# Gate and up columns of the last feed forward as a 2x2 block product in 7 products

## The chip, the cores and the metric

The kernel runs on one core of a Trainium2 chip. The metric is the device time of one execution in microseconds (us). Five engines matter: TensorE (PE in the profile, PEld its weight loads), VectorE (DVE), ScalarE (ACT), GpSimd (POOL) and the queue of SyncE (SPq), which issues the transfers.

## The reference

Two transformer layers on 512 tokens of width 1024, with 256 context tokens. Each layer has a mixer (attention and others) and a feed forward. The change is in the feed forward of layer 1, the last stage of the kernel:

```python
def modulate(x, g, shift, scale):
    return rmsnorm(x, g) * (1.0 + scale) + shift

def swiglu(h, wg, wu, wd):
    return (jax.nn.silu(h @ wg) * (h @ wu)) @ wd
```

Here h is 512 x 1024, wg and wu are 1024 x 2816 (22 column tiles of 128), wd is 2816 x 1024. Everything is f32.

## The kernel before

Activations lie transposed: a tile has 128 features on the partitions and tokens along its length. Every f32 operand of a matmul is split into a high part (H, a cast to fp32r on ACT or POOL) and a low part (L, the rest, a subtraction on DVE), and `mm3` (L141) makes a product of three matmuls: H by H, H by L, L by H. All stages use it.

A weight tile goes through one path. `load` (L122) takes one of four slots of a ring (`wrp`, 128 x 1024 f32) and issues a transfer on SP's queue; `split` (L127) casts it on ACT (L131) and subtracts on DVE (L132). The slot is free once both are done.

The feed forward (`ffn`, L426) goes through the 22 columns in chunks, for layer 1 of 8, 8 and 6 (`CHUNKS1`). For a column j it loads the gate tile wg[j] and the up tile wu[j] (128 x 1024: 8 blocks of 128 x 128, k = 0 to 7), and for each half of the tokens (256 each, `HALVES`) makes gate and up: 2 halves x 2 x 8 x 3 = 96 matmuls of 256 columns. Gate and up of a half share a PSUM bank (`ps_one` for half 0, `ps_tp` for half 1). ACT takes the Silu (L459), DVE multiplies by up (L460), ACT and DVE split the result into aH and aL (L461). The first two columns are interleaved (`lead=2`): both on half 0, then both on half 1. After a chunk of n columns come its 8 down tiles: n x 3 matmuls of 512 columns each into a bank, and a residual on DVE (L322). In the last chunk each residual is followed by the store of that tile.

Ahead of it stands the norm (`last_norm`, L1287), once per half, when the output product of the mixer is done for it (`mix_out`): square sums, a matmul with ones (L279), the reciprocal root, and R, the factor per token in PSUM (L287). `modulated` (L290) then makes for each of 8 k: nt = x R on DVE (L295), scale and shift on ACT (L296), hH on POOL (L297) and hL on DVE (L90). Half 1's norm lies beside the first columns on half 0.

The order of instructions on each engine is set when the program is built, by a scheduler that follows the tile framework's dependences; tiles of a pool are handed round in turn, and each engine runs its instructions in that order.

Of the kernel before, what the change touches and what calls it, by code (L numbers as in the profile page):

```python
# [16 lines left out]
P = 128  # L17
# [24 lines left out]
def trunk(ctx: ExitStack, tc: tile.TileContext, A: dict, out: bass.AP):  # L42
# [23 lines left out]
    def ps_one(shape):  # L66
        return ps.tile(shape, F32, tag="one", name="ps_one", bufs=4)
# [7 lines left out]
    def slot3(dt, name="s3"):  # L75
        return base.tile([P, TT], dt, tag="x3", name=name, bufs=12)
# [12 lines left out]
    def sub(dst, a, H):  # L89
        return dve.tensor_tensor(dst, a, H.bitcast(F32), op=ALU.subtract)  # L90
# [47 lines left out]
    def cut(w, n):  # L138
        return [(w[0][:, 128 * i:128 * i + 128], w[1][:, 128 * i:128 * i + 128]) for i in range(n)]

    def mm3(o, a, b, first, last):  # L141
        (aH, aL), (bH, bL) = a, b
        pe.matmul(o, aH, bH, start=first, stop=False)  # L143
        pe.matmul(o, aH, bL, start=False, stop=False)  # L144
        return pe.matmul(o, aL, bH, start=False, stop=last)  # L145

    waiting, blocks = [], [0]

# [81 lines left out]
    def mod(layer, cond, i):  # L230
        return mods[layer][:, cond, 8 * i:8 * i + 8]
# [40 lines left out]
    def rstd_of(xs, sl, slot=lambda name: slot3(F32, name), between=lambda: None):  # L272

        n = sl.stop - sl.start
        nt = n // 128
        acc = square_sum(xs, sl, slot)
        pt = ps_tp([P, 4, 2])
        for i in range(nt):
            pe.matmul(pt[:, i, :], acc[:, 128 * i:128 * i + 128], ones[:, 0:2], start=True, stop=True)  # L279
        r = small.tile([P, 8], F32, tag="rq", name="rq")  # L280
        between()
        rsqrt(r[:, :nt], pt[:, :nt, 0], 1.0 / 1024, TABR)
        diag = slot("diag")
        for i in range(nt):
            dve.tensor_scalar(diag[:, 128 * i:128 * i + 128], ident, r[:, i:i + 1], None, op0=ALU.mult)
        R = ps_pv([P, 512])
        pe.matmul(R[:, :n], ones, diag[:, :n], start=True, stop=True)  # L287
        return R

    def modulated(xs, sl, R, a, sh, h, ks=range(KT), at=0):  # L290
        n = sl.stop - sl.start
        for k in ks:
            t = slot3(F32, name="nt")
            H, L = h[k][0][:, at:at + n], h[k][1][:, at:at + n]
            dve.tensor_tensor(t[:, :n], xs[k][:, sl], R[:, :n], op=ALU.mult)  # L295
# [130 lines left out]
    def ffn(layer, xs, groups, chunks, last, background=None, grouped=None, ends=None, lead=1, pre=None, nbuf=(2, 1)):  # L426


        off, last_of = 0, []
        nmax = max(n for _, n in chunks)  # L430
        with ExitStack() as own:
            fp = own.enter_context(tc.tile_pool(name=f"ffn{layer}", bufs=1, side="left"))
            more = own.enter_context(tc.tile_pool(name=f"fws{layer}", bufs=1, side="right"))
            turn = [0]

            def ws_unit(src, cols):

                turn[0] += 1
                if (turn[0] - 1) % sum(nbuf) < nbuf[0]:
                    return unit(src, cols, pre, bufs=nbuf[0])  # L440
                return unit(src, cols, more, bufs=nbuf[1])

            def columns(js, acts):
                ws, sgs = [], []
                for j in js:
                    ws.append([cut(ws_unit(A[w + str(layer)][j], 1024), KT) for w in ("wg", "wu")])
                    sgs.append(slot3(F32, name="sg"))
                    acts.append(tuple(fp.tile([P, TT], F32R, tag="a" + x, name="a" + x, bufs=nmax) for x in "HL"))
                for gi, (sl, _, h) in enumerate(groups):
# [12 lines left out]

            for ci, (j0, nj) in enumerate(chunks):
                final = ci == len(chunks) - 1
                if background and final:
                    background.end()
                acts = []
                j = j0
                while j < j0 + nj:
                    js = range(j, j + (lead if j == 0 else 1))  # L470
                    columns(js, acts)
                    j = js.stop
                    if background and j == lead:
                        with tc.issue_after(last_of[1].ins):
                            background.start()
                            background.step()
                    elif background and not final:
                        background.step()

                def wunit(m, unit=ws_unit, **kw):  # L480
                    c = 128 * nj
                    o = (off + m * nj * 128) * 128
                    return cut(unit(A[f"wd{layer}"][o:o + 128 * c].rearrange("(p c) -> p c", p=P), c, **kw), nj)

                def down(pt, w, m, sl, cond):
                    n = sl.stop - sl.start
                    feature_gemm(pt[:, :n], w, [(a[:, sl], b[:, sl]) for a, b in acts])
                    residual(pt[:, :n], xs[m], sl, mod(layer, cond, 5)[:, m:m + 1])

                if final and grouped:  # L490
                    with tc.tile_pool(name=f"fwr{layer}", bufs=1, side="left") as rp:
                        ws = []
                        for gi, (sl, cond) in enumerate(ends):
                            for m in range(KT):
                                if len(ws) <= m:
                                    kw = dict(unit=unit, hp=rp, tag="wd", bufs=KT - sum(nbuf)) if m < KT - sum(nbuf) else {}
                                    ws.append(wunit(m, **kw))
                                down(ps_one([P, 512]), ws[m], m, sl, cond)
                            grouped(gi)
                elif len(groups) == 2 and groups[0][1] == groups[1][1]:  # L500
                    whole = slice(groups[0][0].start, groups[1][0].stop)
                    for m in range(KT):
                        down(ps_one([P, 512]), wunit(m), m, whole, groups[0][1])
                        if final:
                            last(m)
                else:
                    for m in range(KT):
                        w = wunit(m)
                        for sl, cond, _ in groups:
                            down(ps_one([P, 512]), w, m, sl, cond)  # L510
                off += nj * 8 * 128

    def wo_unit(layer, m, hp, bufs):
# [771 lines left out]
    a_ffn = scale_cols(1, 0, 4, "norm_ffn1")  # L1285

    def last_norm(i):  # L1287
        R = rstd_of(xs, HALVES[i])
        h[i] = new_h(1 - i)
        modulated(xs, HALVES[i], R, a_ffn, mod(1, 0, 3), h[i])  # L1290

    banks(3)
    pre1 = ctx.enter_context(tc.tile_pool(name="pre1", bufs=1, side="right"))
    with tc.tile_pool(name="wo1", bufs=1, side="right") as wp:
        mix_out(1, mixs, xs, [(sl, 0, [(H[:, sl], L[:, sl]) for H, L in mixs]) for sl in HALVES], wp, last_norm, wo1)

    def store(m):
        sp.dma_start(out=out[m], in_=xs[m][:, MAIN])

    ffn(1, xs, [(HALVES[i], 0, [(H[:, :256], L[:, :256]) for H, L in h[i]]) for i in range(2)], CHUNKS1, store, lead=2, pre=pre1, nbuf=(4, 1))  # L1300


PARCOLS, ROWCOLS = {}, {}
# [143 lines left out]
```

## Time and profile before

| | |
|---|---|
| median of 3 runs | 1772.79 us (1772.67 to 1772.89) |
| the profiled execution | 1770.36 us, span of its instructions 1768.5 us |
| mean granted TensorE clock | 0.984 |
| PE, DVE, ACT, POOL busy | 1695.4, 945.3, 634.4, 253.3 us |
| last stage (feed forward of layer 1) on PE | from 1392.35 us on |

The times in the profile are those of the one profiled execution, counted from its first instruction. Busy times are sums over the whole span; what a stage costs is read from its own stretch. DVE, ACT and POOL have much idle time in the last stage.

### The profile page before, as it was taken

To read this page: it belongs to the slowest core of one execution; us is meant where nothing else is said; L and a number is where in the kernel's file an instruction comes from. 1 tells how busy PE (TensorE), PEld (TensorE's weight loads), DVE (VectorE), ACT (ScalarE), POOL (GpSimd) and SP (SyncE) were. 2 spreads that over 40 slices of the span, in tenths; PEclk is the share of its full clock that TensorE was granted. 3 is DMA by queue.
4 is the path that set the end of the run, shared out by engine and by line. 5 is a ranking of instruction groups with operands and counts; after the bars stand their busy time and mean duration, and the time that the engine had idled before them with its cause. 6 is when DMAs were issued, how large, how long until landed. Compare 5 with 4: busy or idle time off the path is not lost.

```text
span 1768.5 us, 29065 instructions
## 1 busy us (share of the span) xinstructions
PE 1695.4 (96%) x11590; PEld 1482.4 (84%) x11590; DVE 945.3 (53%) x2072; ACT 634.4 (36%) x1237; POOL 253.3 (14%) x440
## 2 busy tenths in 40 slices
PE   6898999999999999999999999787999999999999
PEld 3687667788888888888889999676878999899897
DVE  5687565646855534533326874558756543333332
ACT  4454454625221221221124643445545432232231
POOL 1341333202000000000001203455221100000000
PEclk9899999999999999999999999898999999999999
DMA  7401324321544423522222222402003032222221
GB/s 267 161 34 52 119 96 143 120 96 54 185 131 154 167 67 124 169 83 72 66 66 93 82 69 72 115 18 69 30 20 132 13 120 96 96 96 96 96 75 57
DMA packets 60662, 171.23 MB, mean 97 GB/s; under 512 B 7152, under 2 KB 14576, under 8 KB 60528
## 3 DMA queue, kind: packets, MB, share of 16 engines
q1 hardware_dynamic: 60528, 169.39, 28.6%
q8 instruction: 91, 1.49, 0.3%
q14 instruction: 43, 0.35, 0.1%
HBM read 160.05 MB, written 4.19 MB: 93 GB/s over the span
## 4 chain that ended last, share of the span: by engine, by line
PE 91%; DVE 4%; DMA 2%; ACT 2%; issue 1%; POOL 1%; SPq 0%; ACTq 0%; POOLq 0%; DVEq 0%
PE ps_one L144 17%; PE ps_one L143 17%; PE ps_one L145 17%; PE ps_tp L394 5%; PE ps_tp L145 5%; PE ps_tp L143 5%; PE ps_tp L144 5%; PE ps_pv L766 3%; PE ps_pv L1229 2%; PE ps_big L143 2%; PE ps_big L145 2%; PE ps_big L144 2%; PE ps_pv L1044 1%; PE ps_big L786 1%; PE ps_pv L143 1%; PE ps_pv L144 1%
## 5 line engine op out<-in xcount | busy, mean ns | idle before, releaser
L131 ACT CAST wH<-wraw 128x1024 fp32r<-128x1024 f32 (+5 forms) x209 | 194.1, 937 | 384.9 <-PE ps_one L144 193.6
L132 DVE TENSOR_TENSOR wL<-wraw,wH 128x1024 fp32r<-128x1024 f32 (+4 forms) x199 | 222.4, 1123 | 170.2 <-ACT wH L131 168.0
L145 PE MATMUL ps_one<-hH,wL 128*128 128x512 f32 (+1 forms) x704 | 236.8, 336 | 0.0
L144 PE MATMUL ps_one<-hL,wH 128*128 128x512 f32 (+1 forms) x704 | 236.7, 336 | 0.0
L143 PE MATMUL ps_one<-hH,wH 128*128 128x512 f32 (+1 forms) x704 | 236.7, 336 | 0.0
L145 PE MATMUL ps_tp<-hH,wL 128*128 128x256 f32 x704 | 196.5, 280 | 0.0
L144 PE MATMUL ps_tp<-hL,wH 128*128 128x256 f32 x704 | 196.3, 279 | 0.0
L143 PE MATMUL ps_tp<-hH,wH 128*128 128x256 f32 x704 | 196.0, 280 | 0.0
L145 PE MATMUL ps_one<-aH,wL 128*128 128x512 f32 (+1 forms) x560 | 194.0, 347 | 0.0
L144 PE MATMUL ps_one<-aL,wH 128*128 128x512 f32 (+1 forms) x560 | 193.9, 347 | 0.0
L143 PE MATMUL ps_one<-aH,wH 128*128 128x512 f32 (+1 forms) x560 | 193.5, 347 | 0.0
L297 POOL TENSOR_SCALAR hH<-nt 128x256 fp32r<-128x256 f32 (+1 forms) x72 | 39.6, 560 | 742.5 <-ACT nt L296 740.5
L145 PEld LDWEIGHTS ps_one<-hH,wL 128*128 128x128 f32 x704 | 132.2, 188 | 15.4
L144 PEld LDWEIGHTS ps_one<-hL,wH 128*128 128x128 f32 x704 | 132.2, 188 | 14.4
L143 PEld LDWEIGHTS ps_one<-hH,wH 128*128 128x128 f32 x704 | 132.3, 188 | 14.2
L387 POOL TENSOR_SCALAR prob<-prob,rs 128x768 f32<-128x768 f32 (+2 forms) x136 | 106.2, 784 | 213.9 <-DVE rs L385 90.1
L143 PEld LDWEIGHTS ps_tp<-hH,wH 128*128 128x128 f32 x704 | 132.3, 188 | 0.9
L144 PEld LDWEIGHTS ps_tp<-hL,wH 128*128 128x128 f32 x704 | 132.0, 188 | 1.0
L145 PEld LDWEIGHTS ps_tp<-hH,wL 128*128 128x128 f32 x704 | 132.3, 188 | 0.1
L143 PEld LDWEIGHTS ps_one<-aH,wH 128*128 128x128 f32 x560 | 105.8, 189 | 14.7
L144 PEld LDWEIGHTS ps_one<-aL,wH 128*128 128x128 f32 x560 | 105.6, 189 | 14.5
L145 PEld LDWEIGHTS ps_one<-aH,wL 128*128 128x128 f32 x560 | 105.5, 188 | 14.5
(300 smaller groups left out, 3548.2 us busy)
## 6 DMA issues: line engine op xcount, KB each, us to landing
wraw<-in_ada_dram SPq DMA_DIRECT2D x80, 512.0 KB, 3.9
wraw<-in_wg_dram SPq DMA_DIRECT2D x44, 512.0 KB, 3.6
wraw<-in_wu_dram SPq DMA_DIRECT2D x44, 512.0 KB, 3.5
wraw<-in_wd_dram SPq DMA_DIRECT2D x32, 384.0 KB, 3.0
wraw<-in_wd_dram SPq DMA_DIRECT2D x16, 512.0 KB, 3.5
wraw<-in_w1n_dram SPq DMA_DIRECT2D x12, 512.0 KB, 3.5
adaw<-in_adaq_dram SPq DMA_DIRECT2D x16, 256.0 KB, 5.4
wraw<-in_adaq_dram SPq DMA_DIRECT2D x8, 512.0 KB, 5.7
```

Of the source, the lines that this page charges most:

```text
L131: act.copy(H, raw[:, :cols])
L132: eng.tensor_tensor(L, raw[:, :cols], H.bitcast(F32), op=ALU.subtract)
L143: pe.matmul(o, aH, bH, start=first, stop=False)
L144: pe.matmul(o, aH, bL, start=False, stop=False)
L145: return pe.matmul(o, aL, bH, start=False, stop=last)
L297: last = (pool.tensor_scalar(H, t[:, :n], 1.0, 1.0, op0=ALU.mult, op1=ALU.mult), sub(L, t[:, :n], H))
L387: pool.tensor_scalar(pr[i], pr[i], r[:, i:i + 1], 1.0, op0=ALU.mult, op1=ALU.mult)
L394: pe.transpose(tp[:, 128 * i:128 * i + 128], b, ident)
L766: pe.matmul(st["pv"][64 * hd:64 * hd + 64, tq], V[kt][:, 64 * kv:64 * kv + 64], pts[hd][:, kt - k0, :], start=kt == k0, stop=kt == 5)
L786: pe.matmul(S[:, ko], Q[:, tq], K[:, ko], start=True, stop=False)
L1044: pe.matmul(o, v[:, hc], pts[hd][:, 2 * (1 - i) + j, :], start=i == 0 and j == 0, stop=i == 1 and j == 1)
L1229: pe.matmul(st["pv"][64 * hd:64 * hd + 64, tq], mV[kt][:, 64 * h:64 * h + 64], pts[hd][:, kt, :], start=kt == 0, stop=kt == 5)
```

## The change

The first two columns stay as they were. For the other 20, gate and up of one column are seen as one 2x2 block product: the rows are gate and up, the inner index is k below 4 (`lo`) and from 4 on (`hi`), and the columns are the two halves of the tokens. It is made in 7 block products (Strassen's, in the form with 15 additions) instead of 8: 7 x 4 x 3 = 84 matmuls of 256 columns per column instead of 96.

What this needs besides: four sums of weight blocks per column (`wsum`, two tiles in the ring `wrp`, made on POOL from the loaded tiles, each half of 128 x 512), which are split like weights; the operands T1 to T4, sums of blocks of the normed h, made once in `last_norm` on DVE and POOL (`tt`) and split (`tH`, `tL`); and additions of the products: some are accumulated in PSUM, three intermediate states of X are copied out by ACT (`snap`), and DVE adds them to the others (`gg`). Silu and the multiplication then follow, the latter on DVE for half 0 and on POOL for half 1. The split weights of a column are gate, s12, s34 (1024 wide) and the upper half of up (512 wide).

The down part is done in chunks of 4, 4, 4, 4, 4 and 2 columns, still with 528 matmuls but with 48 residuals instead of 24.

```diff
-CHUNKS1 = ((0, 8), (8, 8), (16, 6))
+CHUNKS1 = ((0, 4), (4, 4), (8, 4), (12, 4), (16, 4), (20, 2))
...
+    def ffn_fast(layer, xs, halves, h, ops, chunks, last, lead, pre, nbuf):
...
+            def ws(raw, cols=1024):
+                if cols <= 512:
+                    return split(raw, cols, more, tag="wq", bufs=4)
+                hp, n = where()
+                return split(raw, cols, hp, bufs=n)
...
+            def weights(j):
+
+                g, u = (load(A[w + str(layer)][j], 1024) for w in ("wg", "wu"))
+                a1 = cut(ws(g), KT)
+                s12, s34 = (wrp.tile([P, 1024], F32, tag="wr", name="wsum") for _ in range(2))
+                pool.tensor_tensor(s12[:, lo], u[:, lo], u[:, hi], op=ALU.add)
+                pool.tensor_tensor(s12[:, hi], s12[:, lo], g[:, lo], op=ALU.subtract)
+                s12_ = cut(ws(s12), KT)
+                pool.tensor_tensor(s34[:, lo], g[:, lo], u[:, lo], op=ALU.subtract)
+                pool.tensor_tensor(s34[:, hi], g[:, hi], s12[:, hi], op=ALU.subtract)
+                s34_ = cut(ws(s34), KT)
+                a22 = cut(ws(u[:, hi], 512), 4)
+                return a1[:4], a1[4:], a22, s12_[:4], s12_[4:], s34_[:4], s34_[4:]
...
+            def begin(j):
+
+                w = weights(j)
+                X = half_bank(ps_one)
+                sn = slot3(F32, name="snap")
+                product(X, w[0], h[0][:4], True)
+                act.copy(sn[:, 0:256], X)
+                return w, X, sn
+
+            def fast_column(st, nxt, acts):
+                (a11, a12, a22, s1, s2, s3, s4), X, sn = st
+                T1, T2, T3, T4 = ops
+                gg = slot3(F32, name="gg")
+                Y = half_bank(ps_tp)
+                product(Y, s1, T1, True)
+                product(X, s2, T2, False)
+                act.copy(sn[:, 256:512], X)
+                W = half_bank(ps_pv)
+                product(W, a12, h[0][4:], True)
+                dve.tensor_tensor(gg[:, 0:256], W, sn[:, 0:256], op=ALU.add)
+                product(X, s3, T3, False)
+                act.copy(sn[:, 512:768], X)
+                dve.tensor_tensor(gg[:, 512:768], Y, sn[:, 512:768], op=ALU.add)
+                nst = begin(nxt) if nxt is not None else None
+                product(X, a22, T4, False)
+                product(Y, s4, h[1][4:], False)
+                dve.tensor_tensor(gg[:, 256:512], Y, sn[:, 256:512], op=ALU.add)
+                act.activation(gg[:, 0:512], gg[:, 0:512], AF.Silu)
+                dve.tensor_tensor(gg[:, 0:256], gg[:, 0:256], X, op=ALU.mult)
+                pool.tensor_tensor(gg[:, 256:512], gg[:, 256:512], gg[:, 512:768], op=ALU.mult)
+                split_act(new_act(acts), gg[:, 0:512], slice(0, 512))
+                return nst
...
     def last_norm(i):
-        R = rstd_of(xs, HALVES[i])
-        h[i] = new_h(1 - i)
-        modulated(xs, HALVES[i], R, a_ffn, mod(1, 0, 3), h[i])
...
+        raw = []
+        for k in range(4):
+            b = slot3(F32, name="bb")
+            for kk, c in ((k, HALVES[0]), (k + 4, HALVES[1])):
+                dve.tensor_tensor(b[:, c], xs[kk][:, sl], R[:, :256], op=ALU.mult)
+                act.activation(b[:, c], b[:, c], AF.Identity, scale=a_ffn[:, kk:kk + 1], bias=mod(1, 0, 3)[:, kk:kk + 1])
+            bs.append(pair(b[:, :512], group_pair(0, "b"), pool))
+            raw.append(b)
...
+        for k in range(4):
+            b = raw[k]
+            B12, B22 = b[:, HALVES[0]], b[:, HALVES[1]]
+            t = tq.tile([P, 4, 256], F32, tag="t", name="tt", bufs=1)
+            (H11, L11), (H21, L21) = h[0][k], h[0][k + 4]
+            T1, T2, T3, T4 = (t[:, i, :] for i in range(4))
+            dve.tensor_tensor(T1, B12, F(H11), op=ALU.subtract)
+            dve.tensor_tensor(T1, T1, F(L11), op=ALU.subtract)
+            dve.tensor_tensor(T2, B22, T1, op=ALU.subtract)
+            pool.tensor_tensor(T3, B22, B12, op=ALU.subtract)
+            pool.tensor_tensor(T4, F(H21), T2, op=ALU.subtract)
+            pool.tensor_tensor(T4, T4, F(L21), op=ALU.add)
...
-    ffn(1, xs, [(HALVES[i], 0, [(H[:, :256], L[:, :256]) for H, L in h[i]]) for i in range(2)], CHUNKS1, store, lead=2, pre=pre1, nbuf=(4, 1))
+    ffn_fast(1, xs, HALVES, h[:2], h[2], CHUNKS1, store, lead=2, pre=pre1, nbuf=(2, 3))
```

Where it moves instructions, the order on the engines shows it. On DVE, at the norm of half 1 of layer 1's feed forward, there stood before, behind the scaled diagonal that R is made from (L285), the products nt and the low parts hL, then the first activations of column 0 (L460, L90 aL) and the first weight splits:

```order
L285 TENSOR_SCALAR diag<-ident,rq 128x128 x2
L295 TENSOR_TENSOR nt<-xq_14066,ps_pv 128x256
L295 TENSOR_TENSOR nt<-xq_14068,ps_pv 128x256
L295 TENSOR_TENSOR nt<-xq_14070,ps_pv 128x256
L295 TENSOR_TENSOR nt<-xq_14072,ps_pv 128x256
L90 TENSOR_TENSOR hL<-nt,hH 128x256 x2
L295 TENSOR_TENSOR nt<-xq_14074,ps_pv 128x256
...
L460 TENSOR_TENSOR sg<-sg,ps_one 128x256
L90 TENSOR_TENSOR aL<-sg,aH 128x256 x2
L132 TENSOR_TENSOR wL<-wraw,wH 128x1024 x2
```

The same place on DVE now has a split of the upper half of a loaded up tile (L132, 128x512) ahead of the bb's, and behind them T1 and T2 (L1450 to L1452, `tt`), the low parts bL and tL, and weight splits in between:

```order
L132 TENSOR_TENSOR wL<-wraw,wH 128x512
L1438 TENSOR_TENSOR bb<-xq_14066,ps_pv 128x256
L1438 TENSOR_TENSOR bb<-xq_14074,ps_pv 128x256
...
L1450 TENSOR_TENSOR tt<-bb,hH 128x256
L90 TENSOR_TENSOR bL<-bb,bH 128x512
L132 TENSOR_TENSOR wL<-wraw,wH 128x1024
L1451 TENSOR_TENSOR tt<-tt,hL 128x256
L90 TENSOR_TENSOR bL<-bb,bH 128x512
L1452 TENSOR_TENSOR tt<-bb,tt 128x256
L90 TENSOR_TENSOR bL<-bb,bH 128x512 x2
L90 TENSOR_TENSOR tL<-tt,tH 128x512
L559 TENSOR_TENSOR sg<-sg,ps_one 128x256
```

What moved: the low parts of half 1 and the new operands now stand between the weight splits of columns 2 and 3, and the first activation of column 0 (L559, before L460) behind the first pair of T.

On POOL, the last instructions before were the 16 casts hH (8 per half). Now the casts bH of half 1 have four weight sums ahead of them, and T3 and T4 (L1453 to L1455) and further weight sums follow, here up to the second of the four groups of T:

```order
L569 TENSOR_TENSOR wsum<-wraw 128x512
L572 TENSOR_TENSOR wsum<-wraw 128x512
L570 TENSOR_TENSOR wsum<-wsum,wraw 128x512
L573 TENSOR_TENSOR wsum<-wraw,wsum 128x512
L1430 TENSOR_SCALAR bH<-bb 128x512
L1453 TENSOR_TENSOR tt<-bb 128x256
L1430 TENSOR_SCALAR bH<-bb 128x512 x3
L1454 TENSOR_TENSOR tt<-hH,tt 128x256
L1455 TENSOR_TENSOR tt<-tt,hL 128x256
L1453 TENSOR_TENSOR tt<-bb 128x256
L1454 TENSOR_TENSOR tt<-hH,tt 128x256
L1455 TENSOR_TENSOR tt<-tt,hL 128x256
```

What moved: POOL, which had nothing left to do after the norm, has work from here to the end of the kernel.

## Rows read from the trace of the kernel before

**Rows 1.** The page: busy time by engine, and the chain that ended last.

```profile
PE 1695.4 (96%) x11590; PEld 1482.4 (84%) x11590; DVE 945.3 (53%) x2072; ACT 634.4 (36%) x1237; POOL 253.3 (14%) x440
PE 91%; DVE 4%; DMA 2%; ACT 2%; issue 1%; POOL 1%; SPq 0%; ACTq 0%; POOLq 0%; DVEq 0%
```

**Rows 2.** Windows in the last stage: gate and up columns, then down.

```profile
core 0: us, PE busy (x) PEld busy (x) DVE busy (x) ACT busy (x) POOL busy (x), PEclk, DMA share, GB/s
1415.00:1483.00 68.00, 68.00 (x582) 68.00 (x581) 27.27 (x40) 24.02 (x40) 0.00 (x0) 1.00 0.32 109
1483.00:1535.00 52.00, 52.00 (x255) 43.18 (x254) 18.21 (x20) 10.57 (x13) 0.00 (x0) 1.00 0.30 101
```

**Rows 3.** Timeline of ACT: start, duration, what; half 0's Silu of consecutive columns.

```profile
1432.92 0.38 ACT L459 ACTIVATE sg<-ps_one 128x256 f32<-128x256 f32 x1 [2.65 <-PE ps_one L145]
...
1444.17 0.38 ACT L459 ACTIVATE sg<-ps_one 128x256 f32<-128x256 f32 x1 [2.66 <-PE ps_one L145]
```

**Rows 4.** Timeline of PE in the down part, ten matmuls of 512 columns, first and last.

```profile
1488.71 0.40 PE L145 MATMUL ps_one<-aH,wL 128*128 128x512 f32 x1
...
1490.82 0.39 PE L145 MATMUL ps_one<-aH,wL 128*128 128x512 f32 x1
```

**Rows 5.** Timeline of PE, DVE and POOL at the norm of half 1.

```profile
1392.35 0.28 PE L143 MATMUL ps_one<-hH,wH 128*128 128x256 f32 x1
...
1393.63 1.23 DVE L132 TENSOR_TENSOR wL<-wraw,wH 128x1024 fp32r<-128x1024 f32 x1 [0.60 <-ACT wH L131]
1394.77 0.42 DVE L269 TENSOR_TENSOR nacc<-nacc,nsq 128x256 f32<-128x256 f32 x1
...
1403.03 1.41 DVE L295 TENSOR_TENSOR nt<-xq,ps_pv 128x256 f32<-128x256 f32 x4 [3.19 <-PE ps_pv L287]
...
1404.23 2.04 POOL L297 TENSOR_SCALAR hH<-nt 128x256 fp32r<-128x256 f32 x4 [18.90 <-ACT nt L296]
...
1406.26 0.41 DVE L90 TENSOR_TENSOR hL<-nt,hH 128x256 fp32r<-128x256 f32 x1
...
1406.93 0.41 DVE L90 TENSOR_TENSOR hL<-nt,hH 128x256 fp32r<-128x256 f32 x1
```

**Rows 6.** Timeline of POOL and DVE elsewhere, instructions of the shapes that are added.

```profile
83.04 0.73 POOL L326 TENSOR_TENSOR sq<-qn,tabq 128x256 f32<-128x256 f32 x1 [2.91 <-DVE nwm L246]
83.73 0.73 POOL L327 TENSOR_TENSOR sq<-qn,tabq 128x256 f32<-128x256 f32 x1
...
408.22 0.62 POOL L297 TENSOR_SCALAR hH<-nt 128x512 fp32r<-128x512 f32 x1 [0.58 <-ACT nt L296]
...
409.08 0.68 DVE L90 TENSOR_TENSOR hL<-nt,hH 128x512 fp32r<-128x512 f32 x1
409.69 0.47 DVE L322 SCALAR_TENSOR_TENSOR xr<-ps_one,mods,xr 128x256 f32<-128x256 f32 x1
```

**Rows 7.** Timeline of POOL and DVE where both are at work.

```profile
83.82 0.43 DVE L90 TENSOR_TENSOR LA<-ps_tp,KB 64x256 fp32r<-64x256 f32 x1
...
84.51 1.20 DVE L257 SCALAR_TENSOR_TENSOR rq<-nwt,rq 128x8 f32<-128x8 f32 x1
...
84.42 1.27 POOL L328 TENSOR_TENSOR qr<-qn,tabq 128x512 f32<-128x512 f32 x1
...
116.44 2.12 DVE L132 TENSOR_TENSOR wL<-wraw,wH 128x1024 fp32r<-128x1024 f32 x1
...
116.18 1.30 POOL L637 TENSOR_TENSOR d<-win,invc 64x512 f32<-64x512 f32 x1 [0.61 <-DVE win L624]
117.56 2.16 POOL L638 TENSOR_TENSOR d<-d,u 128x512 f32<-128x512 f32 x1
```

**Rows 8.** Timeline of PE behind a wait, and two windows there (columns as in rows 2).

```profile
1122.07 0.58 PE L1078 MATMUL ps_one<-nKA,nQH 128*128 128x256 f32 x1 [3.91 <-ACT prob L383]
...
1124.00:1126.00 2.00, 2.00 (x11) 2.00 (x10) 1.97 (x11) 1.61 (x6) 1.73 (x4) 0.50 0.00 0
1126.00:1128.00 2.00, 2.00 (x16) 1.78 (x14) 1.91 (x8) 1.38 (x5) 1.75 (x5) 0.89 0.36 98
```

**Rows 9.** Loads of line 124 in the last stage, and the last residual.

```profile
DMA to landing us min/median/max: 2.7/3.5/5.4
...
1764.85 0.75 DVE L322 SCALAR_TENSOR_TENSOR xq<-ps_one,mods,xq 128x512 f32<-128x512 f32 x1 [3.46 <-PE ps_one L145]
```

More of the change, by code (lines that the diff above doesn't have):

```diff
@@ L139, in cut, with mm3 @@
         return [(w[0][:, 128 * i:128 * i + 128], w[1][:, 128 * i:128 * i + 128]) for i in range(n)]
-    def mm3(o, a, b, first, last):
+    def mm3(o, a, b, first, last, **kw):
         (aH, aL), (bH, bL) = a, b
-        pe.matmul(o, aH, bH, start=first, stop=False)
-        pe.matmul(o, aH, bL, start=False, stop=False)
-        return pe.matmul(o, aL, bH, start=False, stop=last)
+        pe.matmul(o, aH, bH, start=first, stop=False, **kw)
+        pe.matmul(o, aH, bL, start=False, stop=False, **kw)
+        return pe.matmul(o, aL, bH, start=False, stop=last, **kw)
     waiting, blocks = [], [0]
@@ L510, in ffn, with where, new_act, split_act @@
                             down(ps_one([P, 512]), w, m, sl, cond)
+                off += nj * 8 * 128
+    def ffn_fast(layer, xs, halves, h, ops, chunks, last, lead, pre, nbuf):
+        off = 0
+        nmax = max(n for _, n in chunks)
+        cond = 0
+        whole = slice(halves[0].start, halves[1].stop)
+        with ExitStack() as own:
+            fp = own.enter_context(tc.tile_pool(name=f"ffn{layer}", bufs=1, side="left"))
+            more = own.enter_context(tc.tile_pool(name=f"fws{layer}", bufs=1, side="right"))
+            turn = [0]
+            def where():
+                turn[0] += 1
+                return (pre, nbuf[0]) if (turn[0] - 1) % sum(nbuf) < nbuf[0] else (more, nbuf[1])
+            def ws(raw, cols=1024):
[3 more added lines that the diff above has]
+                return split(raw, cols, hp, bufs=n)
+            def new_act(acts):
+                acts.append(tuple(fp.tile([P, TM], F32R, tag="a" + x, name="a" + x, bufs=nmax) for x in "HL"))
+                return acts[-1]
+            def split_act(act_, v, sl):
+                act.copy(act_[0][:, sl], v)
+                sub(act_[1][:, sl], v, act_[0][:, sl])
+            def plain_columns(js, acts):
+                wts, sgs = [], []
+                for j in js:
+                    wts.append([cut(ws(load(A[w + str(layer)][j], 1024)), KT) for w in ("wg", "wu")])
+                    sgs.append(slot3(F32, name="sg"))
+                    new_act(acts)
+                for gi, sl in enumerate(halves):
+                    for w, sg, a in zip(wts, sgs, acts[-len(js):]):
+                        pm = (ps_one if gi == 0 else ps_tp)([P, 2, 256])
+                        feature_gemm(pm[:, 0, :], w[0], h[gi])
+                        feature_gemm(pm[:, 1, :], w[1], h[gi])
+                        act.activation(sg[:, sl], pm[:, 0, :], AF.Silu)
+                        dve.tensor_tensor(sg[:, sl], sg[:, sl], pm[:, 1, :], op=ALU.mult)
+                        split_act(a, sg[:, sl], sl)
+            lo, hi = slice(0, 512), slice(512, 1024)
+            def weights(j):
[10 more added lines that the diff above has]
+                return a1[:4], a1[4:], a22, s12_[:4], s12_[4:], s34_[:4], s34_[4:]
+            def product(pt, w, b, start):
+                for k in range(4):
+                    mm3(pt, w[k], b[k], start and k == 0, k == 3, skip_group_check=not start)
+            def half_bank(f):
+                return f([P, 512])[:, :256]
+            def begin(j):
[28 more added lines that the diff above has]
+                return nst
+            st = None
+            for ci, (j0, nj) in enumerate(chunks):
+                acts = []
+                js = list(range(j0, j0 + nj))
+                if ci == 0:
+                    plain_columns(js[:lead], acts)
+                    js = js[lead:]
+                    st = begin(js[0])
+                for j in js:
+                    st = fast_column(st, j + 1 if j + 1 < NJ else None, acts)
+                for m in range(KT):
+                    c = 128 * nj
+                    o = (off + m * nj * 128) * 128
+                    w = cut(ws(load(A[f"wd{layer}"][o:o + 128 * c].rearrange("(p c) -> p c", p=P), c), c), nj)
+                    pt = ps_one([P, 512])
+                    feature_gemm(pt, w, acts)
+                    residual(pt, xs[m], whole, mod(layer, cond, 5)[:, m:m + 1])
+                    if ci == len(chunks) - 1:
+                        last(m)
@@ L1287, in last_norm, with pair @@
     def last_norm(i):
-        R = rstd_of(xs, HALVES[i])
-        h[i] = new_h(1 - i)
-        modulated(xs, HALVES[i], R, a_ffn, mod(1, 0, 3), h[i])
+        sl = HALVES[i]
+        R = rstd_of(xs, sl)
+        if i == 0:
+            h[0] = new_h(1)
+            modulated(xs, sl, R, a_ffn, mod(1, 0, 3), h[0])
+            return
+        bs, ops = [], [[], [], [], []]
+        def pair(v, where, eng):
+            H, L = where
+            if eng is act:
+                act.copy(H, v)
+            else:
+                pool.tensor_scalar(H, v, 1.0, 1.0, op0=ALU.mult, op1=ALU.mult)
+            sub(L, v, H)
+            return [(H[:, c], L[:, c]) for c in HALVES]
@@ new lines, in last_norm @@
+        raw = []
[6 more added lines that the diff above has]
+            raw.append(b)
+        h[1] = [p[0] for p in bs] + [p[1] for p in bs]
@@ new lines, in last_norm @@
+        F = lambda x: x.bitcast(F32)
+        for k in range(4):
+            b = raw[k]
[9 more added lines that the diff above has]
+            pool.tensor_tensor(T4, T4, F(L21), op=ALU.add)
+            for i, where in ((0, group_pair(0, "t")), (2, tuple(tq.tile([P, 512], F32R, tag=f"t{x}{k}", name="t" + x) for x in "HL"))):
+                for o, hl in zip(ops[i:i + 2], pair(t[:, i:i + 2, :].rearrange("p a b -> p (a b)"), where, act)):
+                    o.append(hl)
@@ L1292, in trunk @@
+        h.append(ops)
     banks(3)
     pre1 = ctx.enter_context(tc.tile_pool(name="pre1", bufs=1, side="right"))
+    tq = ctx.enter_context(tc.tile_pool(name="tq", bufs=1, side="right"))
     with tc.tile_pool(name="wo1", bufs=1, side="right") as wp:
```

## The prediction

> **What bounds the kernel now.** I read the page first: TensorE (PE) is busy 1695.4 of 1768.5 us, and the chain that ended last is 91% PE [rows 1]. Then the stage that the change rewrites, in windows. One stretch of gate and up columns (1415 to 1483) and one of down products (1483 to 1535) both have PE busy the whole time at a granted clock of 1.00 (the upper level, 2.4 GHz), while DVE has 27 of 68 us of work, ACT 24, POOL none [rows 2]. So here a matmul less is its time less, and what the other engines get to do is free only while PE isn't kept waiting. The reader should see both: the change takes from the bound engine and gives much to an idle one, whose neighbour is DVE.
>
> **Prices of PE.** Two Silu of consecutive columns start 11.25 us apart [rows 3]; a column is 96 matmuls of 256 columns, so one is 0.1172 us. In the down part nine steps take 2.11 us [rows 4], so a matmul of 512 is 0.234 us.
>
> **Term 1, matmuls removed: −28.1 us.** 20 of 22 columns have 84 matmuls instead of 96: 240 × 0.1172 = 28.1. A column is then 9.84 us. The down matmuls keep their number: 528, in 6 chunks instead of 3. The 24 more residuals on DVE (0.75 us each, as the last one in [rows 9]) lie beside PE, whose next tile goes to another bank.
> The Trainium skill, "TensorE: Matmul & The Clock Gate", section on the back-to-back gap, gives N/2.4 GHz + 2.5 ns, 109 ns for 256 columns; by that the term would be an estimated 26.2 us. The row is 117 ns here, and it decides.
>
> **Term 2, the start: +22 us.** The first 7-product column needs T1 to T4, made from half 1's normed values, which themselves come late.
> When does PE need them? In PE's order the last matmul of X·T3 for column 2, the first that needs the second pair of T at k=3, stands about 320 matmuls behind the first one on hH, which started at 1392.35 [rows 5]: without gaps 1392.35 + 320 × 0.1172 = 1429.9.
> When are they there? Before, the first nt stood at 1403.03 and the first hH on POOL at 1404.23 [rows 5]. After, the matmul of the square sums (L279) stands 72 matmuls behind that first one, not 44, because three weight splits of 1024 and one of 512 are ahead of nacc on DVE; that is 3.3 us. Then a split of a just-loaded up tile stands directly ahead of the bb's; that load is issued once its ring slot is free, and takes 3.5 us in the median [rows 9]. I put the first bH at 1409, 5 us later than the first hH.
> From there to the last of the eight tL, DVE has in its order: 12 subtractions of 256 columns for T1 and T2, 4 for aL at 0.335 (1406.26 to 1406.93 is two [rows 5]), 4 bL, 8 tL and 2 weight splits of 512 at 0.61 (409.08 to 409.69 [rows 6]), and 7 weight splits of 1024 at 1.14 (1393.63 to 1394.77 [rows 5]): 5.4 + 8.5 + 8.0 = 21.9 us. POOL has 4 bH at 0.62, 12 operations for T3 and T4 at 0.69 (83.04 to 83.73) [rows 6] and 8 weight sums of 512 at 1.27 (a free POOL instruction of this shape, 84.42 [rows 7]): 2.5 + 8.3 + 10.2 = 21.0 us.
> Do they run beside each other? The rows say no. POOL's 117.56, the same shape as 84.42, took 2.16 us and DVE's split 2.12 instead of 1.23 while they met, and a 128x8 DVE instruction took 1.20 us because POOL's 1.27 us one had begun just before [rows 7]. But DVE's 83.82, which reads one operand from PSUM, took 0.43 us inside POOL's 83.73 [rows 6, 7]. All DVE work counted above reads two SBUF operands, so I take the sum, 21.9 + 21.0 = 42.9: the T's are complete at about 1452, PE waits 22 us, in pieces, for the weight sums of column 3 and for T at k=2 and 3. Lower bound: nothing collides. Then the chain for one k (three on DVE 1.0, two on POOL 1.4, cast and split about 1.2, and hand-overs, since tt has one buffer) is some 4.2 us, four times 17, plus some 10 for bb, bL and sums: 1436, a wait of 6 us. Upper bound 26, a load landing 5.4 us after issue [rows 9] and a little more. I take 22, since the nearest rows are collisions of these very shapes.
> The Trainium skill, "SBUF — State Buffer", section "Who interferes with whom", has the rule behind it: DVE with two SBUF inputs and a GpSimd instruction that reads SBUF exclude each other for the whole instruction, whichever comes first. By it the sum is the serial one, +22; by free overlap it would be +6. The rows agree for pairs; no run here shows 40 us of such work on end.
>
> **Term 3, the clock: +2 us.** After a wait of 3.91 us the granted clock was 0.50 (1.2 GHz) from 1122.07 on and came back in the window from 1126 [rows 8]: some 4 us at half pace lose 2. PE's waits in term 2 are as long. Bounds 0 (the pieces of work between keep it up) and 4 (twice).
>
> **Term 4, the chunks: +4.5 us.** A chunk of four is now 4 × 9.84 on columns plus 96 × 0.234 = 22.5 on down, 61.9 us. Per column POOL has 4 × 1.27 + 0.69 and DVE 3 × 1.14 + 2 × 0.61, excluding each other: 10.4; with 8 down splits 47 of 62 us per chunk, so the mean holds. But both sums live in the same ring of four slots as the raw g and u, so column j+2's loads start only when the POOL sums of an earlier one are done; ACT's casts wait for those loads in order, and the snapshots of X stand behind them on ACT, with 0.3 us or less of slack on PE. I take 1 us per chunk change, 4 to 5 of them; bounds 0 and what rival C gives.
>
> **Term 5, the tail: +3 us.** Before, the last chunk's down began on six tiles' products while the last activation was finished. Now the last column ends in X·T4, the last addition to Y (0.34), Silu of 512 (0.38 for 256 [rows 3], about 0.65), the product on POOL (0.73 [rows 6]), cast and split (1.2), and with two tiles in the chunk less stands ready to cover it. About 3.7 of chain and hand-overs, less 0.7 for a few matmuls. Bounds 0 and 5. The last residual and store stay (1764.85, 0.75 [rows 9]).
>
> **Sum.** The profiled execution took 1770.4 us, 2.4 under the median of the runs. 1770.4 − 28.1 + 22 + 2 + 4.5 + 3 = 1773.8, and with the 2.4 **1776 us**, 0.2% above 1772.8. About 0.2%, 3.5 us, is what a measurement of this kernel can tell from no change.
>
> **Rivals.**
> A (my forecast, 0.46): the start costs what the columns save. Own range 1768 to 1784.
> B (0.20), faster: DVE and POOL get along better than the rows say, or the collisions fall on work that isn't in the chain. The start costs 6 and no clock: 1770.4 − 28.1 + 6 + 4.5 + 3 + 2.4 = 1758. For it: POOL and DVE each have only 21 us, and PE's order puts the T products where the free chain would just have them ready. Against it: [rows 7]. It decides below a wait of some 16 us.
> C (0.26), clearly slower: the ring of four raw slots is too short. A column's cycle is load 3.5 [rows 9], four sums 5.1, and a DVE split ahead of most of them, 3 × 1.14 and a little: 12.4 us, against 9.84 on PE. Only the split weights kept ahead and the 22.5 us of down cover 4 × 2.6 = 10 us per chunk. If 4 us of them stay open in each of five chunks, 20 instead of 4.5: 1792. For it: slots are handed round in order and down loads take them too. Against it: the mean use of 47 of 62 us. It decides from 2 us per chunk on.
> D (0.08), the change does less of both: half of the T work falls into gaps, the wait is 13, 1764 to 1769.
>
> **Range and chances.** From B's middle to C's middle and a little: 1757 to 1795 leaves out half of B and a third of C, under 2 in 10. Faster by over 0.2% (under 1769.2): B, most of D, and a tenth of A, 0.30. Within: a good third of A and rests, 0.23. Slower (over 1776.3): half of A and C, 0.47.
>
> **What would show it.** Term 1: 84 matmuls a column, the distance of two activations 9.8 us in mid-chunk. Term 2: PE idle between 1405 and 1455 adding up to some 22 us, ended by the tH/tL splits and by wL of wsum; POOL's weight sums around 2 us instead of 1.27 where they meet a split. Term 3: a clock under 1.00 behind these waits. Term 4: idle PE at each chunk, ended by snapshots on ACT. Term 5: about 3 us of idle PE ahead of the last down products. I am wrong if POOL's sums keep 1.27 us beside DVE's splits (then B), or if PE waits in mid-chunk for wL of wsum again and again (then C).

## The result: 1.2% slower

The changed kernel took 1793.85 us in the median of four runs (1790.58 to 1795.63), the kernel before 1772.73 (1769.99 to 1772.89): ratio 1.0124, 95% interval 1.0112 to 1.0136. Forecast were 1776 us, in a range of 1757 to 1795. The direction is right, but the forecast's 3 us were, by its own words, no more than what can be told from no change; the loss is 21 us. The time lies outside the forecast's own middle case (A, 1768 to 1784) and where rival C had put it (1792). The range holds it by 1 us, and only because it gave C room.

The page of the profile after, against [rows 1]: PE is busy 3 us less (240 matmuls are gone, but some of the others now run at half the clock and count longer), DVE 113 us more, POOL 159 more, and the chain that ended last lost 13 points of PE to DVE, POOL and transfers.

```profile
PE 1692.0 (94%) x11350; PEld 1470.0 (82%) x11350; DVE 1058.0 (59%) x2196; ACT 685.2 (38%) x1329; POOL 412.5 (23%) x548
PE 78%; DVE 6%; POOL 5%; DMA 5%; issue 2%; ACT 2%; SPq 0%; POOLq 0%; ACTq 0%; DVEq 0%
```

In windows of 10 us, with the columns of [rows 2], the two places where the time went show. The first two rows are the start, the other two a chunk's columns; before, PE was busy in the whole of such windows at 1.00.

```profile
1430.00:1440.00 10.00, 4.57 (x23) 4.36 (x24) 9.88 (x12) 4.29 (x9) 6.06 (x7) 0.70 0.31 106
1440.00:1450.00 10.00, 6.15 (x30) 5.56 (x30) 9.06 (x10) 3.63 (x7) 7.48 (x6) 0.67 0.14 39
...
1510.00:1520.00 10.00, 7.45 (x50) 7.25 (x50) 6.51 (x7) 4.40 (x7) 6.85 (x5) 0.83 0.18 53
...
1580.00:1590.00 10.00, 6.69 (x44) 6.49 (x44) 5.84 (x7) 3.87 (x7) 7.10 (x5) 0.83 0.11 28
```

PE's waits by what ended them (total us, times, longest us), the five longest of 13 groups in this stage. The kernel before has no PE wait there.

```profile
PE ps_tp L143 <- DVE gg L612: 8.3, 4, 3.3
PE ps_tp L143 <- DVE sg L559: 6.4, 2, 3.9
PE ps_tp L143 <- ACT tH L1428: 3.8, 1, 3.8
PE ps_one L143 <- ACT snap L602: 2.0, 2, 1.7
PE ps_one L143 <- DVE gg L614: 1.6, 1, 1.6
```

The three longest waits of the start, one by one:

```profile
1431.56 0.39 PE L143 MATMUL ps_tp<-tH,wH 128*128 128x256 f32 x1 [2.50 <-DVE sg L559]
...
1436.41 0.58 PE L143 MATMUL ps_tp<-tH,wH 128*128 128x256 f32 x1 [3.87 <-DVE sg L559]
...
1445.98 0.58 PE L143 MATMUL ps_tp<-tH,wH 128*128 128x256 f32 x1 [3.78 <-ACT tH L1428]
```

Behind such waits the granted clock fell to 0.50, the lower of its two levels (1.2 GHz). It did so within the second of these, and the next matmuls ran at it. The first window shows that, the second one DVE from the first bb of the start to the end of the last tL:

```profile
1434.00:1440.80 6.80, 4.39 (x20) 4.39 (x21) 6.68 (x10) 3.68 (x7) 4.08 (x4) 0.50 0.41 137
...
1409.89:1452.27 42.38, 30.48 (x191) 28.33 (x190) 39.99 (x52) 22.01 (x38) 27.07 (x24) 0.80 0.14 44
```

To size the stretches I took the start times of all PE matmuls of the stage and subtracted from each step what the matmul costs at full pace (0.1172 and 0.2344 us, [rows 3, 4]). What is left is time lost to waits and to the half clock, in us, in one profiled execution of each kernel. The "start" goes to about 1452 (1472 with four plain columns), the "tail" is the last 20 to 25 us (for e9 the whole last chunk).

| kernel | start | chunks between | tail | all |
|---|---|---|---|---|
| before | – | – | – | 1.4 |
| changed | 21.0 | 24.8 | 4.5 | 50.3 |
| e1, sums in own buffers | 21.4 | 13.9 | 4.5 | 39.8 |
| e2, sums on DVE | 19.9 | 6.0 | 3.1 | 29.0 |
| e3, four plain columns | 7.4 | 17.6 | 3.0 | 28.0 |
| e5, e2 and e3 | 5.4 | 2.4 | 3.1 | 10.9 |
| e7, T3 and T4 on DVE | 23.3 | 20.8 | 3.0 | 47.0 |
| e9, e5, last chunk of 6, a bank more | 6.9 | 1.0 | 1.8 | 9.7 |
| e11, sums and T3, T4 on DVE | 19.6 | 5.5 | 3.1 | 28.1 |

For the change: 50.3 − 1.4 − 28.1 is 20.8 us; the stage also began 2.6 us later (1394.95 against 1392.35), though the program ahead of it is the same. Over the runs of this study that start lay between 1389.9 and 1396.9, so I take it as scatter. Together 23.4, against 23.7 between the two spans.

### The profile page after: what moved, and what is told of

The parts are those of the page before. It is cut to its first block, busy times and chain, and to the rows that moved or that the text cites. A ratio compares the mean times of both kernels' runs of the same rounds, so it can differ in the third digit from the quotient of the medians.

```text
span 1792.2 us, 29101 instructions
## 1 busy us (share of the span) xinstructions
PE 1692.0 (94%) x11350; PEld 1470.0 (82%) x11350; DVE 1058.0 (59%) x2196; ACT 685.2 (38%) x1329; POOL 412.5 (23%) x548
## 4 chain that ended last, share of the span: by engine, by line
PE 78%; DVE 6%; POOL 5%; DMA 5%; issue 2%; ACT 2%; SPq 0%; POOLq 0%; ACTq 0%; DVEq 0%
PE ps_one L143 14%; PE ps_one L144 14%; PE ps_one L145 14%; PE ps_tp L394 5%; DMA wraw<-in_wu_dram 4%; PE ps_pv L893 3%; PE ps_tp L143 3%; PE ps_tp L145 3%; PE ps_tp L144 3%; PE ps_pv L1356 2%; PE ps_big L143 2%; PE ps_big L144 2%; PE ps_big L145 2%; PE ps_pv L143 1%; PE ps_pv L1171 1%
## 5 line engine op out<-in xcount | busy, mean ns | idle before, releaser
L132 DVE TENSOR_TENSOR wL<-wraw,wH 128x1024 fp32r<-128x1024 f32 (+4 forms) x223 | 235.1, 1064 | 141.7 <-ACT wH L131 141.1
L143 PE MATMUL ps_one<-hH,wH 128*128 128x512 f32 (+1 forms) x464 | 170.5, 367 | 0.3 <-ACT wH L131 0.2
L145 PE MATMUL ps_one<-hH,wL 128*128 128x512 f32 (+1 forms) x464 | 170.4, 367 | 0.0
L144 PE MATMUL ps_one<-hL,wH 128*128 128x512 f32 (+1 forms) x464 | 170.0, 366 | 0.0
L378 DVE TENSOR_REDUCE mx<-ps_big 128x1 f32<-128x768 f32 (+1 forms) x92 | 84.6, 921 | 60.6 <-PE ps_big L914 32.5
L1005 DVE CUSTOM_DVE_ANT_0 junk<-wraw,cb 128x1024 f32<-128x1024 f32 x64 | 78.3, 1223 | 50.0 <-DMA wraw<-in_ada_dram 49.5
L394 PE MATMUL ps_tp<-ident,prob 128*128 128x128 f32 x656 | 105.7, 285 | 0.9 <-ACT PT L173 0.7
L143 PEld LDWEIGHTS ps_one<-hH,wH 128*128 128x128 f32 x464 | 87.7, 189 | 15.0 <-ACT wH L131 0.8
L143 PE MATMUL ps_tp<-hH,wH 128*128 128x256 f32 x352 | 98.4, 279 | 0.0
L144 PE MATMUL ps_tp<-hL,wH 128*128 128x256 f32 x352 | 98.4, 279 | 0.0
L145 PE MATMUL ps_tp<-hH,wL 128*128 128x256 f32 x352 | 98.2, 279 | 0.0
```

The source lines that it names most:

```text
L132: eng.tensor_tensor(L, raw[:, :cols], H.bitcast(F32), op=ALU.subtract)
L143: pe.matmul(o, aH, bH, start=first, stop=False, **kw)
L144: pe.matmul(o, aH, bL, start=False, stop=False, **kw)
L145: return pe.matmul(o, aL, bH, start=False, stop=last, **kw)
L378: dve.reduce_max(mx[:, :nh], S, axis=AX)
L394: pe.transpose(tp[:, 128 * i:128 * i + 128], b, ident)
```

## The experiments

**e1: buffers of their own for the weight sums.** The ring then holds raw tiles alone.

```diff
-                s12, s34 = (wrp.tile([P, 1024], F32, tag="wr", name="wsum") for _ in range(2))
+                s12, s34 = (more.tile([P, 1024], F32, tag="wsum", name="wsum", bufs=2) for _ in range(2))
```

> The weight sums get two buffers of their own, so the ring of four holds raw tiles alone; work, engines and order of operations are the same. Theory R (the ring): a column's loads no longer wait for the four POOL sums of the column before, so of the 23 us lost in the chunks behind the first some 4 stay: 1794 - 19 = about 1775 us; the start (21 us) stays. Rival L (the exclusion of DVE and POOL itself slows the columns) and rival K (chunks of four cost it at their edges): nothing of it depends on where the sums lie, 1790 to 1796 us.

Measured: 1781.05 us, ratio to before 1.0051 (1.0035 to 1.0067). Between the expectations: the chunks lose 13.9 instead of 24.8 and the start is unchanged. The ring is the cause of nearly half of the chunks' loss (10.9 of 24.8), and something else of the rest.

How the ring does it shows in the changed kernel's chain of waits from 1496 on (start, us, what). It goes round: the last sum of a column frees the slot of the next up tile, whose load takes 3.5 to 4.2 us, four sums follow, and so on.

```profile
1496.78 1.31 POOL wsum L573
...
1498.11 3.54 DMA wraw<-in_wu_dram
...
1501.81 1.30 POOL wsum L569
1503.11 0.07 issue
1503.17 1.62 POOL wsum L570
1504.79 2.23 POOL wsum L572
1507.02 1.70 POOL wsum L573
1508.72 0.02 issue
1508.74 4.17 DMA wraw<-in_wu_dram
1512.91 0.02 issue
1512.94 0.63 ACT wH L131
1513.56 0.02 issue
1513.59 1.29 DVE wL L132
1514.88 0.35 DVE gg L612
1515.23 0.04 issue
1515.27 0.39 PE ps_tp L143
```

The end of it is worth a look: the wait is put down to `gg`, L612, a short addition that frees a bank. But that addition had only stood in DVE's queue behind a weight split, that behind its cast on ACT, and that behind the load. In the next chunk the loads of up tiles are issued at these times on SP's queue, one per column:

```profile
1546.05 0.33 SPq L124 DMA_DIRECT2D wraw<-in_wu_dram  x1
...
1557.43 0.33 SPq L124 DMA_DIRECT2D wraw<-in_wu_dram  x1
...
1566.92 0.33 SPq L124 DMA_DIRECT2D wraw<-in_wu_dram  x1
...
1577.22 0.33 SPq L124 DMA_DIRECT2D wraw<-in_wu_dram  x1
```

The steps are 11.4, 9.5 and 10.3 us, against PE's 9.84 a column. Over the four chunks behind the start such steps are 9.2 to 12.6 us, 10.7 in the mean; in e1 they are 3.7 to 9.2. So with the sums in it the ring is on average a little slower than PE needs, and never gets ahead.

**e2: the sums on DVE.** Four lines, of which the first is shown; the ring is as in the change.

```diff
-                pool.tensor_tensor(s12[:, lo], u[:, lo], u[:, hi], op=ALU.add)
+                dve.tensor_tensor(s12[:, lo], u[:, lo], u[:, hi], op=ALU.add)
...
```

> The four weight sums of a column are made on DVE instead of POOL, in the same ring. Theory R: between the loads of two columns then lie four sums of about 0.61 us instead of four of 1.3 to 2.2, the cycle load 3.5 + 2.5 + hand-overs is 7 us and below the 9.84 of PE: the chunks lose some 4 instead of 23. At the start DVE has 8 x 0.61 more and POOL 10 us less in the serial sum, 5 us off the 21: about 1794 - 19 - 5 = 1770 us. Rival L gives much the same, since the sums and the splits can't collide any more. Rival K: only the start gains, about 1789 us. Against all: DVE gets 45 of 62 us per chunk; if it is late then, 1785 or more.

Measured: 1773.02 us, ratio 1.0007 (0.9996 to 1.0018), some 21 us less than the change: theory and rival L share the hit. The chunks now lose 6.0. The start gained 1 us, not 5. What the sums on POOL did to DVE is read from the groups of DVE's splits of 128x512 behind the start, first in the changed kernel, then with the sums on DVE (busy, mean ns):

```profile
L132 DVE TENSOR_TENSOR wL<-wraw,wH 128x512 fp32r<-128x512 f32 x55 | 52.5, 964 | 34.2 <-ACT wH L131 33.9
```

```profile
L132 DVE TENSOR_TENSOR wL<-wraw,wH 128x512 fp32r<-128x512 f32 x55 | 37.2, 687 | 25.2 <-ACT wH L131 25.2
```

In the changed kernel the sums themselves took 1.51 to 1.68 us in the mean, the longest group being

```profile
L569 POOL TENSOR_TENSOR wsum<-wraw 128x512 f32<-128x512 f32 x17 | 28.5, 1676 | 91.0 <-DMA wraw<-in_wu_dram 74.7 <-DVE wL L132 7.3 <-issue 4.9
```

against 1.27 alone [rows 7], and on DVE in e2

```profile
L569 DVE TENSOR_TENSOR wsum<-wraw 128x512 f32<-128x512 f32 x17 | 11.7, 688 | 8.6 <-DMA wraw<-in_wu_dram 8.6
```

So the rest after e1 goes when the sums leave POOL. The longer splits speak for rival L, but a sum on POOL also takes nearly twice as long as one on DVE when nothing holds it up (1.27 against 0.69 us), and no run takes these two apart. In e1, with buffers of their own, the sums slowed the splits even more (1017 ns in the mean for 128x512), and in the middle of a chunk one split of 1024 took 2.35 us instead of 1.23:

```profile
1499.28 2.35 DVE L132 TENSOR_TENSOR wL<-wsum,wH 128x1024 fp32r<-128x1024 f32 x1
```

**e3: four plain columns first.** In two pairs; the first chunk is then plain.

```diff
-                    plain_columns(js[:lead], acts)
+                    for q in range(0, lead, 2):
+                        plain_columns(js[q:q + 2], acts)
                     js = js[lead:]
-                    st = begin(js[0])
+                    st = begin(lead)
...
-    ffn_fast(1, xs, HALVES, h[:2], h[2], CHUNKS1, store, lead=2, pre=pre1, nbuf=(2, 3))
+    ffn_fast(1, xs, HALVES, h[:2], h[2], CHUNKS1, store, lead=4, pre=pre1, nbuf=(2, 3))
```

> Four plain columns at the start instead of two (two pairs), so the first chunk is wholly plain and 18 columns use 84 matmuls. T1 to T4 are needed some 40 us later. Theory (the 21 us at the start are the serial chain of DVE and POOL work up to the T's): 24 more matmuls cost 2.8 us, the wait for T goes, the one for bH and bL (some 4 us between 1410 and 1420) stays: 1794 - 21 + 4 + 2.8 = 1780 us, between 1776 and 1784. Rival: the wait is handed on to the first columns behind chunk 0, since their weight sums lie in the same ring: 1788 or more.

Measured: 1777.30 us, ratio 1.0027 (1.0012 to 1.0041). As the theory expected, the wait for T was not handed on: the start loses 7.4 instead of 21.0, and the chunks lose less too, 17.6 us, with one chunk fewer behind the start.

**e4: the short chunks alone**, in the kernel before (`CHUNKS1` of the change, nothing else).

> The kernel before with the chunks of the change (4, 4, 4, 4, 4, 2) and nothing else of it. Rival K (the edges of short chunks cost the time): 5 us or more over the kernel before, 1778 to 1795. Theory R: 24 more residuals and smaller down loads lie beside PE, within 1 us: 1773 us.

Measured: 1771.37 us, ratio 1.0000 (0.9991 to 1.0010). Rival K is out: in the kernel before, where no weight is late, the edges cost nothing.

**e5: e2 and e3 together.**

> Both edits together: weight sums on DVE, and four plain columns at the start. Theory (the loss has two separate parts, the start with T and the ring with POOL's sums in the chunks): of the 29 us that PE still waits or runs slow with the sums on DVE, the 20 at the start become some 9 with lead 4 (7.4 in the first chunk and 1.6 behind it), for 2.8 us of matmuls: 1773 - 11 + 3 = 1765 us, between 1761 and 1768, faster than before. Rival (the parts share their time, one hides behind the other): 1770 or more.

Measured: 1758.45 us, ratio 0.9922 (0.9907 to 0.9936), faster than the kernel before and 6.5 us better than the theory's sum, below its 1761 to 1768. The two parts don't hide behind each other; each is smaller with the other's edit: the start loses 5.4 instead of 7.4 in e3, the chunks 2.4 instead of 6.0 in e2. PE's waits in the whole stage are now:

```profile
PE ps_tp L144 <- DVE bL L90: 2.3, 2, 1.5
PE ps_one L143 <- DVE gg L614: 1.8, 2, 1.6
PE ps_one L143 <- ACT snap L607: 0.9, 2, 0.5
PE ps_tp L143 <- POOL bH L1431: 0.4, 1, 0.4
```

**e6: e5 with the sums' own buffers** (the edit of e1).

> As the run with both edits, and the sums in two buffers of their own as well. Theory: with the sums on DVE the ring's cycle is shorter than a column on PE already, so the room is worth little, 0 to 2 us: 1763 to 1765 us. Rival (the ring still holds up loads, mostly at the chunks' edges): 4 us or more faster than without, 1761 or less.

Measured: 1757.87 us, ratio 0.9921 (0.9904 to 0.9937). Within 1 us of e5. The intervals could hide 2 us, but the traces agree: the chunks lose 2.3 us here and 2.4 in e5. With sums of 0.69 us on DVE the ring of four is long enough.

**e7: T3 and T4 on DVE**, sums on POOL as in the change.

```diff
-            pool.tensor_tensor(T3, B22, B12, op=ALU.subtract)
-            pool.tensor_tensor(T4, F(H21), T2, op=ALU.subtract)
-            pool.tensor_tensor(T4, T4, F(L21), op=ALU.add)
+            dve.tensor_tensor(T3, B22, B12, op=ALU.subtract)
+            dve.tensor_tensor(T4, F(H21), T2, op=ALU.subtract)
+            dve.tensor_tensor(T4, T4, F(L21), op=ALU.add)
```

> Only T3 and T4 move from POOL to DVE (12 operations at the start); the weight sums stay on POOL. By the serial sum of the prediction the start gets 12 x 0.69 us of POOL less and 12 x 0.335 of DVE more: 4 us less, 1790 us. Rival (DVE's own queue sets the start; while it is never idle POOL's work costs only where it blocks a DVE instruction): 0 to 3 us more or less, 1792 to 1797 us.

Measured: 1790.24 us, ratio 1.0101 (1.0084 to 1.0118). The time is what the serial sum expected, and yet the sum is wrong: the start loses 23.3 us, 2 more than in the change, as the rival says. In the profiled run the gain came from elsewhere: the stage began 4.4 us earlier (1390.57, scatter), and chunks and tail lost 5.5 less. The total of one kernel can't tell such theories apart, the stretch can.

**e11: sums, T3 and T4 all on DVE**, two plain columns (e2 and e7 together).

> Weight sums and T3, T4 all on DVE, two plain columns as in the change: POOL keeps only the four bH at the start. By the serial sum of the prediction the start has 18.5 us of POOL less and 8.9 of DVE more: 9.6 us less than 21, some 11 to 12 us left, 1764 us. Theory now (DVE's own queue is the bound from 1410 on, with bb, the activations of the plain columns and the additions that the sum left out; POOL cost it some 12 us in which its instructions were blocked): 27 + 4.9 + 4.1 = 36 us of DVE instead of 39, so 18 to 20 us stay at the start, 1771 us, and DVE is still busy all the time there.

Measured: 1772.43 us, ratio 1.0007 (0.9995 to 1.0018); the start loses 19.6 us with POOL empty but for four bH. Windows of the start:

```profile
1410.00:1420.00 10.00, 8.41 (x52) 7.47 (x51) 9.72 (x19) 6.04 (x12) 3.66 (x4) 0.83 0.00 0
1420.00:1430.00 10.00, 10.00 (x88) 10.00 (x87) 9.40 (x20) 7.42 (x12) 0.00 (x0) 1.00 0.01 2
1430.00:1440.00 10.00, 2.60 (x19) 2.10 (x17) 10.00 (x20) 3.74 (x8) 0.00 (x0) 0.74 0.39 131
1440.00:1450.00 10.00, 8.05 (x33) 7.31 (x34) 8.23 (x16) 5.14 (x9) 0.00 (x0) 0.50 0.20 52
```

The theory's 18 to 20 us hold, the serial sum's 11 to 12 don't. DVE is busy 37 of these 40 us: its queue bounds the start, here with the work that came from POOL, in the change with what POOL's work blocked. And the last of the T's is not what the start's loss hangs on. Here its split (tL) ended at 1447.9, in the changed kernel at 1452.3, though the stage began 1.9 us later here; and still the start lost only 1.4 us less. First e11 (the last two splits in one row), then the changed kernel:

```profile
1446.43 1.46 DVE L90 TENSOR_TENSOR tL<-tt,tH 128x512 fp32r<-128x512 f32 x2
```

```profile
1451.59 0.68 DVE L90 TENSOR_TENSOR tL<-tt,tH 128x512 fp32r<-128x512 f32 x1
```

**e8: the last two chunks as one of 6**, on e5 (`CHUNKS1` with (16, 6) at its end).

> Sums on DVE, lead 4, and the last two chunks (4 and 2) made one of 6, so that five tiles stand ready for the down products while the last column's activation is made. Theory (the tail's 3 to 4.5 us come from the short last chunk): 2.5 to 4 us less than the run with both edits, about 1762 us. Rival (the tail waits for the last column in any case): within 1 us of it.

Measured: 1758.49 us, ratio 0.9917 (0.9895 to 0.9939). The rival holds: no gain over e5. The times alone could hide the theory's 2.5 to 4 us, but chunks and tail together lose 5.4 us in this trace and 5.5 in e5's. The wait in the tail stayed, and it is for a bank, the one that X of the last column holds until it is multiplied (L614):

```profile
PE ps_one L143 <- DVE gg L614: 2.1, 1, 2.1
PE ps_one L143 <- ACT snap L607: 1.4, 1, 1.4
```

**e9: a bank of another pool for the fourth down tile of the last chunk**, on e8.

```diff
-                    pt = ps_one([P, 512])
+                    pt = (ps_pv if ci == len(chunks) - 1 and m == 3 else ps_one)([P, 512])
```

> As the run with the last chunk of 6, and its fourth down tile in a bank of the other pool (ps_pv). Theory (the tail's wait of 2.1 us is for the bank that X of the last column holds until it is multiplied): the fourth tile starts without it, and 15 matmuls of 512 columns, 3.5 us, cover the rest: about 2 us less than that run, 1756 us. Rival (the order of ACT and DVE sets the tail, the wait moves to the next tile or to aL): within 1 us of it, 1758 us.

Measured: 1754.90 us, ratio 0.9908 (0.9893 to 0.9924), the lowest median of all; the intervals of e5, e6, e8, e9 and e10 overlap, so the times alone don't show the 2 us. The trace does: the wait on L614 is gone; of the waits behind the start one is left:

```profile
PE ps_one L143 <- ACT snap L607: 0.9, 1, 0.9
```

**e10: T1 to T4 written behind the first pair of plain columns**, on e9: the loop over `tt` in `last_norm` becomes a function, called by `ffn_fast`.

```diff
+                        if q == 0:
+                            ops = ops()
...
```

> As the run with the bank, and T1 to T4 written behind the first pair of plain columns instead of ahead of it. Theory (of the 5 us still lost in the first chunk, the T work between the bL's on DVE and POOL makes a part; the rest is R that comes 3 us later behind weight splits): 1 to 3 us less, 1753 to 1755 us. Rival (DVE fills its gaps with T in either order): the same within 1 us.

Measured: 1756.32 us, ratio 0.9918 (0.9904 to 0.9932). The rival holds, the start loses 6.8 as before. What makes these 5 to 7 us is only argued: R comes later than in the kernel before, behind weight splits, and two waits for bL are followed by some us at half clock. It was not taken apart further.

## Why the prediction came out as it did

- **Term 1, −28.1: right.** With 240 matmuls fewer at the full pace of 0.1172 us, the account above closes to 0.3 us.
- **Term 2, +22, and term 3, +2: the total came out, the working did not.** Start and clock cost 21.0 us instead of 24. PE's waits, counted from start to start, are some 16 of it and the half clock some 5. So term 2 was too large, and term 3 beyond its bound of 4: the clock was at 0.50 in three stretches of the start, 17 us together. That the errors offset each other was luck.
- **Term 2, the first step that failed: "I take the sum, 21.9 + 21.0 = 42.9".** From the first bb (1409.89) to the end of the last tL (1452.27; the forecast said 1452) DVE was busy 40.0 of 42.4 us. Undisturbed its instructions there would take 26.6 us: the 21.9 of the sum and 4.7 for bb, the activations and the additions of W, which the sum had left out. So POOL blocked DVE for some 13 us, not for all of its 21. That the end still fell on 1452 was luck too: what was left out, and a first bH at 1411.58 instead of 1409, made up for the shorter blocking.
- **Term 2, the second: what PE waits for.** The forecast had it wait for the weight sums of column 3 and for T, until the last T was there. Of the three long waits two ended with L559, the multiplication of a plain column. It reads a bank of `ps_tp` that PE needs next, and it had stood in DVE's queue behind T work and weight splits. Only the third ended with a T. Behind it PE did not wait again in the start, though the last tL ended 6 us later.
- **Rival B's bound was not tested.** e2 and e11 show what POOL's work at the start is worth when DVE gets it: the start loses 1 to 1.4 us less. No run has the start without collisions and without more work on DVE. DVE's 26.6 us alone, from 1409.89 on, would end at 1436.5, close to the 1436 that the lower bound of 6 us stands on.
- **Term 4, +4.5: the step that failed most.** It measured 24.8. "The mean holds, 47 of 62 us" proves nothing here, since the work is a cycle and not a pile: load, four sums, next load. Rival C had the cycle as its reason, and with 4 us per chunk nearly its size (4 to 7 in each of four chunks). Its price of 12.4 us a column was too high, the issues of the loads show 10.7 in the mean. About half of the loss is the ring (e1); the other half went when the sums left POOL (e2), where the rows show them and the splits slowing each other; the short additions and snapshots that PE waits for stand queued behind such work. What of it is the collision and what a sum's longer time on POOL alone was not taken apart. The chance of 0.26 for C was too low, because I set a mean against it and didn't follow the slots through one chunk.
- **Term 5, +3: right in kind.** 4.5 us. The forecast put it on the chain of the last activation; e8 and e9 show that 2 us of it are a PSUM bank that this chain frees.
- **The rule on the exclusion.** The Trainium skill, "SBUF — State Buffer", section "Who interferes with whom", says that the later of the two instructions waits for the whole of the other. The rows agree in direction (964 against 687 ns in the mean for a split with the sums on POOL and on DVE). What the forecast made of it, two serial sums, did not follow: a POOL instruction costs DVE only what is left of it when DVE wants to start. Where DVE reads one operand from PSUM no cost shows: the last two bb's took 0.41 us each, as the others did, while bH and T3 ran on POOL from 1411.58 on.

## What to carry to other kernels

Fewer matmuls on a bound engine are worth their time only if the operands that replace them arrive a stage ahead; here 28 us were saved and 49 given back. Before trusting a mean load, follow one buffer ring through one round: what frees the slot, how long the load then takes, and what must be computed before the next slot is free. Give sums to the engine that makes them shortest (0.69 us on DVE against 1.3 to 2.2 on POOL beside it), and start the new scheme only where its operands are ready; with both (e5), the same idea is 0.8% faster than the kernel before.

## What the runs showed of the hardware

GpSimd's 128x512 sums, 1.27 us alone, took 1.51 to 1.68 us in the mean beside DVE's splits, and 1.67 to 1.99 with buffers of their own, while DVE's splits of that shape went from 964 to 1017 ns: more room made the instructions slower and the kernel faster. On DVE such a sum took 0.69 us. The runs of the kernel before lay between 1767.5 and 1775.8 us over the study, and the last stage of kernels with the same program ahead of it began up to 7 us apart. So single profiles of this kernel can't settle 5 us, but the lost time of one stage can be compared.
